# A two-layer attention trunk: compression with both halves stationary, rotary columns once, and weight halves made by GpSimd

## The chip, the core and the metric

One core of a Trainium2 chip runs the whole program. Its engines are TensorE (PE, matrix products; PEld is its weight load), VectorE (DVE), ScalarE (ACT) and GpSimd (POOL); SyncE (SP) issues nearly all transfers from HBM. Each engine takes its instructions strictly in order and waits at an instruction until the semaphores it needs are set. The metric is the device time of one execution in microseconds (us); lower is better.

## What is computed

Two layers over a residual stream of 256 rows by 1024 columns, all in float32. The part of a layer that the change touches is its first, the token mixing; cross-attention over 256 memory rows and a gated FFN with a short convolution follow.

```
h = x @ w_in[l]
cq, ckv, kr, nq, kc, vc, ks, vs, kw, vw, gl = split(h)
# latent attention: 8 heads of 64 plain + 32 rotary columns
q = (rms_norm(cq, cq_g) @ w_uq).reshape(B, S, 8, 96)
q_rope = apply_rope(q[..., 64:], cos, sin)
# sparse attention: 8 heads in 2 groups; its compressed branch
flat = overlapping blocks of 32 rows (stride 16) of kc or vc, plus a position code
kc_, vc_ = gelu(flat @ w1 + b1) @ w2          # 15 blocks, 2 groups, 64 columns
s = q @ kc_.T * scale - slope * distance;  p_c = masked_softmax(s)
o = g0 * (p_c @ vc_) + g1 * selected_branch + g2 * window_branch
mix = concat(o_mla, o_nsa) @ w_out[l];  x = LN(alpha * x + mix)
```

## The kernel before

A float32 product is made of three fast ones: each operand is split into a rounded part hi and a rest lo, and hi*hi + hi*lo + lo*hi are summed in PSUM. So every weight goes through the same steps (`piece`): a transfer into a raw tile, hi by ScalarE (L130), lo = raw - hi by VectorE (L131), and the matmuls. A piece is up to 128 x 1024; there are 4 raw tiles and 6 of hi and of lo. `wmat` cuts a weight into pieces, `mm_nat` (L169 to L171) and `mm_tr` (L177 to L179) issue the three products.

The program is a list of steps for each layer (`attn` in the table CFG). Layer 0 runs: kc, nq1, nq0, par, k, cmp, v, mem, tab, qk0, cq, qk1, cps, ckv, cmt, fill and so on. The list only sets the order in which the steps are written; a scheduler then puts each engine's instructions in an order of its own, which mixes steps. What matters here:

- kc projects the inputs of the compression and splits them into c2 (hi and lo, tiles of their own). cmp (`compress`) multiplies them by w1: for each of two branches (key, value) and 8 slices three matmuls with 34 stationary columns (32 blocks and 2 of the position code) and 256 moving ones (L516 to L518). The result hs (34 x 512) is copied from PSUM by VectorE (L160; the table's option H is 0), transposed in four pieces (L523), copied to ht, and a gelu by its tanh form follows: u, u2, a tanh on ScalarE (L540). gek and gev (L542, L547) are its results; two products with w2 (L552, L554) make the compressed keys kc and values vct.
- v projects values and gates; cq and ckv are the low-rank query and key inputs of the latent attention.
- mem normalizes the two tiles of 128 memory rows, mb: mean and spread by VectorE (or, for one tile, ScalarE), the power -0.5 on GpSimd (`rsqrt`, L209, tiles mv and ss), then on VectorE (x - mean) * g (L239) and times the power plus b (L240), each in two halves of 512 columns.
- tab loads six tables. GpSimd makes the distance table alibi for 8 heads out of neg (L323), 8 instructions.
- cps makes the probabilities of the compressed branch: 32 products of 32 columns (cmps), steps on VectorE, and on GpSimd a subtraction (L657) and a mask (L659). They are stored 32 wide, of which 16 hold values, the rest is set to zero by GpSimd (L667). cmt transposes them in 4 pieces (L675); in av0 to av3 the products with vct (L690) take 32 rows each.
- mq0 to mq3 (`mla_q`) make the query of two heads each. The 32 rotary columns stand twice in the weight, the second time with halves swapped, so that a head fills 128 columns; one multiplication by the table c_cs (L749) evicts both heads, and the score product adds the two rotary parts. That is 18 matmuls of 256 columns for each of four steps.
- fill is work for the next stage (keys and values of the cross-attention, out of the normalized memory), put in where TensorE might wait. pt and pT are transposed attention probabilities, qk the scores.

Of the kernel before, what the change touches and what calls it, by code (L numbers as in the profile page):

```python
# [53 lines left out]
def consts():  # L54
# [1007 lines left out]
```

## Time and profile before

| | us |
|---|---|
| median of 3 runs | 880.95 |
| lowest, highest | 879.26, 881.2 |
| the profiled execution, its own time | 879.98 |
| its span, first to last instruction | 877.9 |
| TensorE busy, share of the span | 860.3, 98% |
| VectorE, ScalarE, GpSimd busy | 665.2, 532.5, 132.4 |
| mean granted TensorE clock, of full speed | 0.993 |

The profile is of one execution; it begins at its first instruction, and 2.1 us of the time lie outside the span. Matmuls are pipelined: the duration of one record (280 ns for 256 columns) is longer than the distance to the next, and only the distance adds to the time. "L" and a number is a line of the kernel. A time in square brackets is how long an engine idled ahead of the row, with what ended the wait. A step on PSUM or SBUF that reads what another engine wrote waits for that engine's semaphore, and all that stands behind it in its queue waits with it.

### The profile page before, as it was taken

Reading aid. Unit: us, or ns where it says so; the run is one execution under the profiler, and the core shown is the slowest. Engines: PE = TensorE matmul, PEld = TensorE weight load, DVE = VectorE, ACT = ScalarE, POOL = GpSimd, SP = SyncE. Lnnn points to the kernel's source line nnn. Section 1 sums busy time; section 2 is a strip of 40 time slices with the busy share of each in tenths; the row PEclk is TensorE's granted clock in tenths of the full one; section 3 lists DMA queues with packets and bytes.
Section 4 is the critical chain, followed back from the end, with each engine's and each line's share of the span. In section 5 each row is a group of like instructions: output and inputs, shape, how many; then the busy total and the mean of one; then the engine's idle time right before and its main releaser. Section 6 shows DMA issues by size and latency. Waiting matters only on the chain.

```text
span 877.9 us, 14948 instructions
## 1 busy us (share of the span) xinstructions
PE 860.3 (98%) x5502; PEld 766.7 (87%) x5502; DVE 665.2 (76%) x1290; ACT 532.5 (61%) x1014; POOL 132.4 (15%) x140
## 2 busy tenths in 40 slices
PE   8989999999999999999999999999999999999996
PEld 5989798899989888888989998879998888888895
DVE  7789887766578877677688788968566877777777
ACT  5658764555546676666555678636573567667661
POOL 1052000000000332222300020000000033223220
PEclk9989999999999999999999999999999999999998
DMA  7944463476347756656538634446633655665641
GB/s 229 284 145 124 132 173 113 140 251 190 96 123 237 217 158 216 190 165 217 183 110 239 190 90 110 144 127 210 194 119 121 218 159 179 212 192 171 215 142 48
DMA packets 128236, 148.66 MB, mean 169 GB/s; under 512 B 6259, under 2 KB 111009, under 8 KB 128163
## 3 DMA queue, kind: packets, MB, share of 16 engines
q1 hardware_dynamic: 128159, 147.70, 54.5%
q8 instruction: 43, 0.70, 0.3%
q14 instruction: 30, 0.25, 0.1%
q10 hardware_dynamic: 4, 0.01, 0.0%
HBM read 146.64 MB, written 1.05 MB: 168 GB/s over the span
## 4 chain that ended last, share of the span: by engine, by line
PE 91%; DVE 4%; ACT 2%; DMA 2%; issue 1%; POOL 0%; SPq 0%; DVEq 0%; ACTq 0%; POOLq 0%
PE up L259 16%; PE up L261 8%; PE acc L996 5%; PE acc L997 5%; PE acc L998 5%; PE acc L170 3%; PE acc L171 3%; PE acc L169 3%; PE fill L178 2%; PE fill L179 2%; PE xq L179 2%; PE xq L178 2%; PE xq L177 2%; PE fill L171 2%; PE fill L169 2%; PE fill L170 2%
## 5 line engine op out<-in xcount | busy, mean ns | idle before, releaser
L131 DVE TENSOR_TENSOR lo<-raw,hi 128x1024 fp32r<-128x1024 f32 (+5 forms) x296 | 322.8, 1108 | 96.2 <-ACT hi L130 94.0
L130 ACT ACTIVATE hi<-raw 128x1024 fp32r<-128x1024 f32 (+5 forms) x296 | 275.8, 951 | 108.9 <-PE acc L171 34.4
L259 PE MATMUL up<-xT,hi 128*128 128x512 f32 x608 | 152.1, 392 | 0.0
L259 PEld LDWEIGHTS up<-xT,hi 128*128 128x128 f32 x608 | 110.3, 189 | 20.3
L261 PEld LDWEIGHTS up<-xT,lo 128*128 128x128 f32 x608 | 82.9, 190 | 5.9
L984 POOL TENSOR_TENSOR cv<-cv 128x256 f32<-128x256 f32 x40 | 54.2, 1356 | 218.7 <-ACT cv L982 170.0
L261 PE MATMUL up<-xT,lo 128*128 128x256 f32 x608 | 84.8, 282 | 0.0
L978 ACT ACTIVATE cv<-u,par 128x256 f32<-128x256 f32 x76 | 45.4, 598 | 49.6 <-DVE u L971 49.6
L996 PE MATMUL acc<-hi,frh 128*128 128x512 f32 x176 | 68.9, 392 | 0.0
L997 PE MATMUL acc<-lo,frh 128*128 128x512 f32 x176 | 68.8, 391 | 0.0
L998 PE MATMUL acc<-hi,frl 128*128 128x512 f32 x176 | 68.2, 389 | 0.0
L209 POOL TENSOR_TENSOR mv<-mv,mhalf 128x1 f32<-128x1 f32 x16 | 14.3, 897 | 309.0 <-DVE mv L233 158.5
L979 DVE SCALAR_TENSOR_TENSOR cv<-u,par,cv 128x255 f32<-128x255 f32 x76 | 37.6, 495 | 26.4 <-ACT cv L978 26.4
L584 ACT ACTIVATE p<-p,nm 128x128 f32<-128x128 f32 x96 | 42.6, 447 | 9.7 <-DVE nm L581 9.4
L986 ACT ACTIVATE frh<-cv 128x256 fp32r<-128x256 f32 x44 | 18.4, 418 | 37.8 <-POOL cv L984 35.4
L987 POOL TENSOR_TENSOR frl<-cv,frh 128x256 fp32r<-128x256 f32 x40 | 38.0, 952 | 20.3 <-ACT frh L986 20.3
L980 DVE SCALAR_TENSOR_TENSOR cv<-u,par,cv 128x254 f32<-128x254 f32 x76 | 37.9, 498 | 2.5
L998 PEld LDWEIGHTS acc<-hi,frl 128*128 128x128 f32 x176 | 33.0, 188 | 7.5 <-DVE frl L987 0.7
L996 PEld LDWEIGHTS acc<-hi,frh 128*128 128x128 f32 x176 | 33.1, 188 | 7.0 <-ACT frh L986 0.9
L997 PEld LDWEIGHTS acc<-lo,frh 128*128 128x128 f32 x176 | 33.1, 188 | 6.0
L177 PE MATMUL fill<-mTh,hi 128*128 128x256 f32 x128 | 37.2, 291 | 0.0
L179 PE MATMUL fill<-mTh,lo 128*128 128x256 f32 x128 | 36.6, 286 | 0.0
(279 smaller groups left out, 2151.7 us busy)
## 6 DMA issues: line engine op xcount, KB each, us to landing
raw<-in_ffn_w_up SPq DMA_DIRECT2D x88, 512.0 KB, 4.4
raw<-in_ffn_w_down SPq DMA_DIRECT2D x44, 512.0 KB, 4.3
raw<-in_xa_wkv SPq DMA_DIRECT2D x32, 512.0 KB, 3.8
raw<-in_xa_wq SPq DMA_DIRECT2D x16, 512.0 KB, 5.4
raw<-in_xa_wo SPq DMA_DIRECT2D x16, 512.0 KB, 4.2
raw<-in_w_in SPq DMA_DIRECT2D x24, 256.0 KB, 3.4
raw<-in_w_out SPq DMA_DIRECT2D x16, 256.0 KB, 4.6
raw<-in_w_out SPq DMA_DIRECT2D x8, 512.0 KB
```

Source lines behind the costliest of these rows:

```text
L130: A.activation(h_, x_, AF.Copy)
L131: V.tensor_tensor(l_, x_, h_.bitcast(F32), op=ALU.subtract)
L169: T.matmul(o, xh_[:, t, k], h, start=k == 0, stop=False)
L177: T.matmul(o, h[:, ms], xh_[:, :, k], start=k == 0, stop=False)
L179: T.matmul(o, lo[:, ms], xh_[:, :, k], start=False, stop=k == len(ws) - 1)
L259: T.matmul(o, h[:, ms], x2[:, k], start=k == 0, stop=False)
L261: T.matmul(o[:, 0:S], lo[:, ms], x2[:, k, 0], start=False, stop=k == len(ws) - 1)
L978: A.activation(c, u, AF.Identity, bias=pcol("cb", l, ft), scale=w_[2])
L984: E.tensor_tensor(conv[0], conv[0], conv[1], op=ALU.mult)
L996: T.matmul(o, fh[:, ts_], h[:, cs_], start=f == 0, stop=False)
L997: T.matmul(o, fh[:, ts_], lo[:, cs_], start=False, stop=False)
L998: T.matmul(o, fl[:, ts_], h[:, cs_], start=False, stop=f == NF - 1)
```

## The change

Four things change in the token mixing of both layers; nothing else does.

1. **Compression.** hi and lo of the inputs lie side by side in one tile, and both are stationary at once, 68 columns in place of 34. Two matmuls for each slice do what three did, 64 in place of 96 in all. (The product lo*lo comes along.) hs has 68 rows, is copied by ScalarE (option H is 1), and its transposes have 68 columns each; ht takes ScalarE's copy of the lo part and an addition on VectorE.
2. **Compressed branch.** Keys and probabilities are 16 wide, all heads of both groups in one set of 128 rows: one value product in place of two (a layer), vct spread over heads by a multiplication with a new table c_half, two transposes in place of four, and no zeroing of the probabilities. The products with vct have 128 rows in place of 32.
3. **Query.** The rotary columns stand once. Each step makes 9 matmuls for the plain columns of two heads; every second step makes 9 more for the rotary columns of four. The eviction is by ScalarE copies for the plain part; for the rotary part by a shuffle, three VectorE steps on 128 x 256 and four copies. c_cs has twice the size. GpSimd clears 32 rows of each query tile.
4. **GpSimd makes lo halves.** In cq, ckv, mkv and fill every second piece's lo is GpSimd's, in mq0 to mq3 every one (L135 and L760 of the new file).

The order of the last steps of the lists becomes mq0 mq1 ... mq2 mq3 in both layers.

```diff
+        share["n"] += share["on"]
+        E = G if share["on"] and share["n"] % 2 else V
...
-            V.tensor_tensor(l_, x_, h_.bitcast(F32), op=ALU.subtract)
+            E.tensor_tensor(l_, x_, h_.bitcast(F32), op=ALU.subtract)
...
+            call = big.tile([P, 2, 2, 272], F32R, name="c2", tag="oTh")
             for j, nm in ((0, "pek"), (1, "pev")):
-                ch, cl = [tmp.tile([P, 272], F32R, name="c2" + s_, tag="pp", bufs=PP) for s_ in "hl"]
+                c = call[:, j]
+                ch, cl = c[:, 0], c[:, 1]
...
-                        o = hid[0:34, j * 256:(j + 1) * 256]
-                        c_h, c_l = ch[:, i:i + 265:8], cl[:, i:i + 265:8]
-                        T.matmul(o, c_h, h[:, i - i0], start=i == 0, stop=False)
-                        T.matmul(o, c_h, lo[:, i - i0], start=False, stop=False)
-                        T.matmul(o, c_l, h[:, i - i0], start=False, stop=i == 7)
+                        o = hid[0:68, j * 256:(j + 1) * 256]
+                        c_hl = c2[j][:, :, i:i + 265:8]
+                        T.matmul(o, c_hl, h[:, i - i0], start=i == 0, stop=False)
+                        T.matmul(o, c_hl, lo[:, i - i0], start=False, stop=i == 7)
...
-            A.activation(ht.rearrange("p a b c -> p (a b c)"), pt[:, 0:136], AF.Copy)
+            A.activation(htf, hp[:, :, 1], AF.Copy)
+            V.tensor_tensor(htf, hp[:, :, 0], htf, op=ALU.add)
...
-            for g in range(2):
-                T.matmul(pc[:, 128 + g * 64:192 + g * 64], gv[:, g].rearrange("p i b -> p (i b)"), w2[:, 2, :],
-                         start=True, stop=True)
+            T.matmul(pc[:, 128:192], gv.rearrange("p j g b -> p (j g b)"), w2[:, 2, :], start=True, stop=True)
...
+            V.tensor_tensor(vct, pc[:, None, 128:192].to_broadcast([P, HN, 64]),
+                            half[:, :, None].to_broadcast([P, HN, 64]), op=ALU.mult)
...
-            pc = st.tile([P, NT, HN, 32], F32, name="pc", tag="pc", bufs=1)
-            G.memset(pc, 0.0)
-            V.tensor_tensor(pc.rearrange("p t h b -> p (t h) b")[:, :, 0:16], f, bc(mx), op=ALU.mult)
+            V.tensor_tensor(f, f, bc(mx), op=ALU.mult)
...
-            for g in range(2):
-                for t in range(NT):
-                    T.transpose(pt[:, g * S + t * P:g * S + (t + 1) * P],
-                                pc[:, t, 4 * g:4 * g + 4, :].rearrange("p h b -> p (h b)"), ident)
+            for t in range(NT):
+                T.transpose(pt[:, t * P:(t + 1) * P], pc[:, t * P:(t + 1) * P], ident)
...
-                T.matmul(po[64 * g:64 * g + 64, 0:S], vct[js, g, :], pct[js, g, :], start=False, stop=True)
+                T.matmul(po[64 * g:64 * g + 64, 0:S], vct[:, 2 * j + g, :], pct, start=False, stop=True)
...
-            for i in range(2):
-                mm_tr(pb[:, i * S:(i + 1) * S], ch[0], ch[1], ws, i * P)
-            j = 2 * (hp % 2)
-            V.tensor_tensor(qT[hp // 2][:, j:j + 2, :], pb.rearrange("p (i n) -> p i n", i=2),
-                            cs[:, None, :].to_broadcast([P, 2, S]), op=ALU.mult)
+            for cut, dh, dl in ((slice(0, 64), h, lo), (slice(64, 96), rh[:, :, ms], rl[:, :, ms])):
+                src, dh, dl = heads(rv)[:, :, :, cut], heads(dh), heads(dl)
+                A.activation(dh, src, AF.Copy)
+                G.tensor_tensor(dl, src, dh.bitcast(F32), op=ALU.subtract)
+            mm_tr(pb[:, 0:S], ch[0], ch[1], [(h[:, k], lo[:, k]) for k in range(3)], 0)
+            if last:
+                mm_tr(pb[:, S:2 * S], ch[0], ch[1], [(rh[:, k], rl[:, k]) for k in range(3)], 0)
+            for j in range(2):
+                A.activation(qT[g][0:64, 2 * i + j, :], pb[64 * j:64 * j + 64, 0:S], AF.Copy)
+            if last:
+                V.stream_shuffle(rs, pb[:, S:2 * S], [(c + 16) % 32 for c in range(32)])
+                V.tensor_tensor(rc, pb[:, S:2 * S], cs[:, 0], op=ALU.mult)
+                V.tensor_tensor(rs, rs, cs[:, 1], op=ALU.mult)
+                V.tensor_tensor(rc, rc, rs, op=ALU.add)
+                for j in range(4):
+                    copy_(qT[g][64:96, j, :], rc[32 * j:32 * j + 32], j % 2)
...
+                for g in range(2):
+                    G.memset(qT[g][96:128], 0.0)
+            share["on"] = name in ("cq", "ckv", "mkv", "fill") or name[:2] == "mq"
```

The scheduler's order shifts with it. The places that matter, in layer 0; numbers behind a name tell tiles of one kind apart. TensorE, from the end of the v projection (proj, 280 columns) to the start of cq (384 columns), before:

```order
L170 MATMUL proj_655<-lo_624,xT_103 128x280
L171 MATMUL proj_655<-hi_623,xT_103 128x280
L169 MATMUL proj_829<-hi_807,xT_103 128x384
L170 MATMUL proj_829<-lo_808,xT_103 128x384
L552 MATMUL cmp_597<-gek_587,w2_593 128x30
L554 MATMUL cmp_597<-w2_593,gev_589 128x64 x2
L171 MATMUL proj_829<-hi_807,xT_103 128x384
```

and now:

```order
L174 MATMUL proj_638<-lo_607,xT_103 128x280
L561 MATMUL cmp_581<-gek_571,w2_577 128x30
L175 MATMUL proj_638<-hi_606,xT_103 128x280
L562 MATMUL cmp_581<-w2_577,gev_573 128x64
L251 MATMUL lnt_685<-c_ident_80,mb_668 128x128 x4
L173 MATMUL proj_812<-hi_790,xT_103 128x384
```

The product with gek has moved up by three matmuls, ahead of the last of the v projection. VectorE, the steps that lead to gek, before (mb is the memory, mv its norms, u2 the gelu's argument):

```order
L239 SCALAR_TENSOR_TENSOR mb_685<-mb_685,mv_716,mg_686 128x512
L538 TENSOR_SCALAR u2_582<-u2_582 128x60
L239 SCALAR_TENSOR_TENSOR mb_685<-mb_685,mv_716,mg_686 128x512
L539 TENSOR_TENSOR u2_582<-u2_582,u_575 128x60
L229 TENSOR_SCALAR mv_691<-mv_691 128x1
L239 SCALAR_TENSOR_TENSOR mb_685<-mb_685,mv_691,mg_686 128x512 x2
L542 SCALAR_TENSOR_TENSOR gek_587<-u2_582,u_575 128x30
```

and now:

```order
L244 SCALAR_TENSOR_TENSOR mb_668<-mb_668,mv_699,mg_669 128x512
L546 TENSOR_TENSOR u2_566<-u_559 128x60
L243 SCALAR_TENSOR_TENSOR mb_668<-mb_668,mv_699,mg_669 128x512
L547 TENSOR_SCALAR u2_566<-u2_566 128x60
L233 TENSOR_SCALAR mv_674<-mv_674 128x1
L243 SCALAR_TENSOR_TENSOR mb_668<-mb_668,mv_674,mg_669 128x512
L548 TENSOR_TENSOR u2_566<-u2_566,u_559 128x60
L244 SCALAR_TENSOR_TENSOR mb_668<-mb_668,mv_674,mg_669 128x512
L551 SCALAR_TENSOR_TENSOR gek_571<-u2_566,u_559 128x30
```

Two steps L244 (L240 before), which multiply by the power, now stand ahead of gek; before, all of that kind stood behind it. GpSimd, from the alibi steps to the compressed probabilities sc, before:

```order
L323 TENSOR_SCALAR alibi_179<-neg_744 128x256 x8
L209 TENSOR_TENSOR mv_716<-mv_716,mhalf_84 128x1
L209 TENSOR_TENSOR mv_691<-mv_691,mhalf_84 128x1
L544 MEMSET gev_5641 128x256
L209 TENSOR_TENSOR ss_855<-ss_855,mhalf_84 128x1
L209 TENSOR_TENSOR ss_886<-ss_886,mhalf_84 128x1
L657 TENSOR_TENSOR sc_954<-sc_954,cmx_957 128x256
L209 TENSOR_TENSOR ss_1013<-ss_1013,mhalf_84 128x1
L659 TENSOR_TENSOR sc_954<-sc_954,c_cok_178 128x256
```

and now:

```order
L328 TENSOR_SCALAR alibi_180<-neg_727 128x256 x8
L213 TENSOR_TENSOR mv_699<-mv_699,mhalf_84 128x1
L135 TENSOR_TENSOR lo_791<-raw_788,hi_790 128x768
L213 TENSOR_TENSOR mv_674<-mv_674,mhalf_84 128x1
L553 MEMSET gev_5606 128x128
L135 TENSOR_TENSOR lo_803<-raw_800,hi_802 128x768
L135 TENSOR_TENSOR lo_953<-raw_950,hi_952 128x864
L135 TENSOR_TENSOR lo_965<-raw_962,hi_964 128x576
L213 TENSOR_TENSOR ss_838<-ss_838,mhalf_84 128x1
L213 TENSOR_TENSOR ss_869<-ss_869,mhalf_84 128x1
L665 TENSOR_TENSOR sc_937<-sc_937,cmx_940 128x256
L135 TENSOR_TENSOR lo_1058<-raw_1055,hi_1057 128x1024
```

Halves of weights stand between the two powers of the memory, and one of 1024 columns between the two steps of the probabilities. On SyncE's queue, the fifth piece of w_in, 512 KB, was issued ahead of the layer's parameters and now is issued behind them; neg follows later in the same queue in both.

## Rows read from the trace of the kernel before

**Rows 1.** page, 1: engine, busy us (share), instructions; 4: the chain's shares

```profile
PE 860.3 (98%) x5502; PEld 766.7 (87%) x5502; DVE 665.2 (76%) x1290; ACT 532.5 (61%) x1014; POOL 132.4 (15%) x140
...
PE 91%; DVE 4%; ACT 2%; DMA 2%; issue 1%; POOL 0%; SPq 0%; DVEq 0%; ACTq 0%; POOLq 0%
```

**Rows 2.** TensorE's waits: engine line <- what ended it: us, times, longest

```profile
PE cmp L523 <- DVE hs L160: 4.0, 2, 3.2
...
PE pt L597 <- ACT pT L600: 1.4, 3, 0.6
```

**Rows 3.** stretches: us, busy us of PE, PEld, DVE, ACT, POOL, clock, DMA share, GB/s

```profile
20.00:30.00 10.00, 10.00 (x86) 10.00 (x85) 7.98 (x15) 5.94 (x12) 0.00 (x0) 1.00 0.97 262
...
46.30:50.70 4.40, 1.28 (x11) 1.05 (x8) 4.28 (x8) 3.06 (x5) 4.40 (x5) 0.88 0.88 271
...
52.00:54.00 2.00, 2.00 (x10) 2.00 (x10) 2.00 (x10) 1.50 (x3) 1.94 (x2) 0.50 0.84 245
54.00:56.50 2.50, 2.50 (x13) 2.50 (x12) 2.50 (x7) 1.04 (x5) 2.27 (x4) 0.51 0.68 227
...
500.00:502.00 2.00, 1.23 (x11) 1.17 (x11) 1.79 (x6) 0.29 (x1) 0.00 (x0) 1.00 0.92 243
```

**Rows 4.** timeline of TensorE, layer 0: start, us, engine, line, op, out<-in

```profile
50.77 0.64 PE L523 MATMUL cmp<-c_ident,hs 34*128 34x34 f32 x4 [3.18 <-DVE hs L160]
...
59.24 0.30 PE L552 MATMUL cmp<-gek,w 128*128 128x30 f32 x2
...
84.50 0.60 PE L675 MATMUL cmpt<-c_ident,pc 128*128 128x128 f32 x4
84.85 0.36 PE L177 MATMUL fill<-mTh,hi 128*128 128x256 f32 x1
```

**Rows 5.** stretch of the compression's matmuls alone: us, busy (x), clock, DMA, GB/s

```profile
40.70:46.30 5.60, 5.60 (x48) 1.00 0.96 308
```

**Rows 6.** timelines of SyncE's queue and of GpSimd, layer 0

```profile
38.76 0.51 SPq L321 DMA_DIRECT2D neg<-in_c_neg  x1
...
45.03 10.03 POOL L323 TENSOR_SCALAR alibi<-neg 128x256 bf16<-128x256 f32 x8 [32.32 <-DMA neg<-in_c_neg]
55.14 1.28 POOL L209 TENSOR_TENSOR mv<-mv,mhalf 128x1 f32<-128x1 f32 x2
...
77.49 0.63 POOL L657 TENSOR_TENSOR sc<-sc,cmx 128x256 f32<-128x256 f32 x1 [3.42 <-DVE cmx L655]
...
79.98 0.73 POOL L659 TENSOR_TENSOR sc<-sc,c_cok 128x256 f32<-128x256 f32 x1
```

**Rows 7.** timeline of VectorE, layer 0

```profile
50.03 0.68 DVE L160 COPY hs<-cmp 34x512 f32<-34x512 f32 x1
...
58.17 0.19 DVE L542 SCALAR_TENSOR_TENSOR gek<-u,u 128x30 f32<-128x30 f32 x1 [1.50 <-ACT u L540]
58.27 0.34 DVE L547 SCALAR_TENSOR_TENSOR gev<-u,u 128x60 f32<-128x60 f32 x2
58.54 0.75 DVE L240 SCALAR_TENSOR_TENSOR mb<-mb,mv,mg 128x512 f32<-128x512 f32 x1
```

**Rows 8.** groups by form: line, engine, op, tiles, x; busy us, mean ns

```profile
L984 POOL TENSOR_TENSOR cv<-cv 128x256 f32<-128x256 f32 x40 | 54.2, 1356 | 218.7 <-ACT cv L982 170.0 <-PE up L259 48.7
L987 POOL TENSOR_TENSOR frl<-cv,frh 128x256 fp32r<-128x256 f32 x40 | 38.0, 952 | 20.3 <-ACT frh L986 20.3
...
L435 POOL TENSOR_TENSOR kr<-m 128x32 f32<-128x32 f32 x4 | 1.6, 404 | 6.1 <-DVE m L433 6.1
L657 POOL TENSOR_TENSOR sc<-sc,cmx 128x256 f32<-128x256 f32 x2 | 1.3, 626 | 51.2 <-DVE sm L588 47.8 <-DVE cmx L655 3.4
...
L131 DVE TENSOR_TENSOR lo<-raw,hi 128x1024 fp32r<-128x1024 f32 x228 | 280.5, 1240 | 93.5 <-ACT hi L130 91.4 <-PE up L963 0.7
```

More of the change, by code (lines that the diff above doesn't have):

```diff
@@ L73, in consts @@
     ok = np.broadcast_to(ok, (P, NT, HN, 16))
-    ctab = np.where(ok, -(slopes * 8.0)[None, None, :, None] * (t - cend), -BIG).astype(f)
+    order = np.arange(HN).reshape(2, 4).T.reshape(-1)
+    ctab = np.where(ok, -(slopes[order] * 8.0)[None, None, :, None] * (t - cend), -BIG).astype(f)
+    half = np.repeat(0.5 * np.eye(HN, dtype=f), 16, 0)
     return {
-        "c_ident": ident, "c_neg": neg, "c_tri": tri, "c_cs": cs, "c_kcs": np.ascontiguousarray(kcs),
+        "c_ident": ident, "c_neg": neg, "c_tri": tri, "c_cs": np.ascontiguousarray(cs), "c_kcs": np.ascontiguousarray(kcs),
@@ L115, in trunk @@
     RAW, HL, PP = SIZES
+    share = {"on": False, "n": 0}
     def piece(nk, n, segs, wn=None, cols=None):
@@ L316, in trunk @@
     cok = const.tile([P, NT, HN, 16], F32, name="c_cok", tag="c_cok")
+    half = const.tile([P, HN], F32, name="c_half", tag="c_half")
     alibi = const.tile([P, HN, S], BF16, name="alibi", tag="alibi")
@@ L745, in mla_q @@
-            pb = bank("mla")
-            for i in range(2):
-                mm_tr(pb[:, i * S:(i + 1) * S], ch[0], ch[1], ws, i * P)
-            j = 2 * (hp % 2)
-            V.tensor_tensor(qT[hp // 2][:, j:j + 2, :], pb.rearrange("p (i n) -> p i n", i=2),
-                            cs[:, None, :].to_broadcast([P, 2, S]), op=ALU.mult)
+            g, i = divmod(hp, 2)
+            last = g in rw
+            if not last:
+                rw[g] = [wp.tile([P, 3, P], F32R, name="r" + s, tag=s, bufs=HL) for s in ("hi", "lo")]
@@ new lines, in mla_q @@
+            rh, rl = rw[g]
+            r = wp.tile([P, 1024], F32, name="raw", tag="raw", bufs=RAW)
+            rv = r[:, :576].rearrange("p (k n) -> p k n", k=3)
+            nc.sync.dma_start(rv, a["mla_w_uq"][l][:, hp * 192:(hp + 1) * 192].rearrange("(k p) n -> p k n", p=P))
+            h, lo = [wp.tile([P, 3, P], F32R, name=s, tag=s, bufs=HL) for s in ("hi", "lo")]
+            heads = lambda v: v.rearrange("p k (h c) -> p k h c", h=2)
+            ms = slice(64 * i, 64 * i + 64)
+            for cut, dh, dl in ((slice(0, 64), h, lo), (slice(64, 96), rh[:, :, ms], rl[:, :, ms])):
+                src, dh, dl = heads(rv)[:, :, :, cut], heads(dh), heads(dl)
+                A.activation(dh, src, AF.Copy)
+                G.tensor_tensor(dl, src, dh.bitcast(F32), op=ALU.subtract)
@@ L794, in trunk @@
             "ckv": in_ckv,
-            "par": lambda: load_params((0,)),
+            "par": lambda: (load_params((0,)), nc.sync.dma_start(half, a["c_half"])),
             "par2": lambda: load_params((1, 2, 3)),
```

54 lines of the change are left out of this document (26 added, 28 removed).

## The prediction

> **What bounds the kernel now.** First the busy table and the chain of work that ended last [rows 1]: TensorE is busy for 860.3 of 877.9 us and carries 91% of the chain; GpSimd is busy for 15% and carries none of it. So a matmul that goes is worth its spacing wherever TensorE's queue is full, and nothing where the next instruction waits for another engine. Next, TensorE's list of waits [rows 2]: the largest by far is the four transposes of the compression's hidden layer, which wait for hs, 4.0 us in two places, 3.2 of it in layer 0. The windows round that place [rows 3] show a second price: the granted clock is 1.00 in 20 to 30 us, 0.88 while TensorE idles, and 0.50 from 52 to 54, that is 1.2 in place of 2.4 GHz, after the engine had stood; layer 1's shorter wait at 500 leaves 1.00. Last, the timelines of TensorE, GpSimd and VectorE from 45 to 60 us [rows 4, 6, 7], since that is where the change puts new instructions into queues that are served in order.
>
> **Direct savings on TensorE.** Compression: 48 matmuls of 256 columns fill 5.60 us of a layer [rows 5], 0.117 us each; 16 of 48 go, 1.9 us in each layer. The query: 72 become 54 a layer, and I take the same size of matmul at the same spacing: 18 x 0.117 = 2.1 us a layer. The transposes of the compressed probabilities: four stand from 84.50 to 84.85 [rows 4], 0.09 us each, two go, 0.2. The value product behind gek loses two of four matmuls, shorter still; at the same price 0.2. The eight products with 128 rows in place of 32 keep their number and their columns. Sum 4.4 us a layer, 8.8 in all, 1.0% of the time. Now what lies behind each.
>
> **Layer 0, to the start of cq.** Before, hs is copied by VectorE at 50.03 [rows 7], behind pieces of weights, and its transposes start at 50.77 after 3.18 us of idling [rows 4]. ScalarE now copies it, behind the key evictions only, so up to 3.2 us of idling, up to 2.8 us of slow clock (some 5.7 us at half rate, from 50.8 to 56.5 [rows 3, 4]), the 1.9 of the compression and about 0.5 at the start (the first piece's lo no longer stands ahead of x) become free: TensorE would reach the end of the v projection near 50.5 in place of 58.9. But the product with gek stands ahead of the last v matmul, in TensorE's order. gek is now behind five steps that normalize the memory, on VectorE; two of these (L244) wait for GpSimd's powers, and those stand behind eight alibi steps. Before, gek came ahead of all steps that need a power, at 58.17, and VectorE took the first of them at 58.54 [rows 7].
> By rows, with the table neg landing as before: alibi 45.03 to 55.06 [rows 6]; the first power 0.64 (1.28 for two), to 55.8; on VectorE then three mb steps of 0.75 and four small ones that follow each other at 0.1 as gek and gev do (58.17, 58.27) [rows 7], to 58.5; GpSimd meanwhile a lo half of 768 columns and the second power. That half has no row on GpSimd. The nearest: a plain two-operand step of 128x32 takes 404 ns and one of 128x256 with an fp32r result 952 [rows 8]; that is 2.45 ns a column and 326 ns fixed, 2.2 us for 768. So power two ends near 58.7, mb takes 0.75, gek 0.19, and TensorE goes on near 59.8. The equal point before is L552's start at 59.24 [rows 4] less two cq matmuls of 384 columns ahead of it (1.5 x 0.117 each): 58.9. So 0.9 late. Besides, 512 KB of w_in that were issued ahead of the parameters are now issued behind them, and neg's issue at 38.76 [rows 6] is behind that: at 262 GB/s [rows 3] 2.0 us if no hole in the DMA takes them up, 0 if all; I take 1.0. So +1.9 (bounds 0.3 to 2.9). TensorE has then stood some 9 us, longer than the 3.2 after which the clock was at half; I take the same 2.8 us of slow running, now under cq (bounds 0 and 2.8). Layer 0 stands at **+4.7** where cq is under way, and the compression's gain, the wait's and the start's are in it already.
>
> **Layer 0, the rest.** The value product gives 0.2 and the query 2.1 back; the compressed probabilities lose 0.2 of transposes. Their chain has a new link: GpSimd's subtraction (77.49) and its mask (79.98) [rows 6] now have a whole lo half of 1024 between them, 2.45 x 1024 + 326 ns = 2.8 us. Before, a power stood there, and TensorE idled 1.4 us in all for pT [rows 2], some of it at this place. The transposes now stand ahead of 48 fill matmuls that could have covered for them. I take +1.2 (bounds -1 and +3). VectorE loses the lo halves (a 1024 one takes 1240 ns there [rows 8]), and so some of its lateness; the bound of -1 is for that. The query's lo halves of 384 and 192 columns (1.3 and 0.8 us), the shuffle and the rotary steps run while TensorE has other heads' work queued: nothing. Layer 0: 4.7 - 2.5 + 1.2 = **+3.4**.
>
> **Layer 1.** No alibi and no memory norm stand in the way here. The 4.4 are saved; hs stands behind ScalarE's two key copies, I take 0.5 more wait than the 0.8 of before (4.0 less 3.2 [rows 2]), since TensorE arrives 1.9 earlier at a copy that starts little earlier (bounds -0.8 and +1.4), and 0.5 for two powers of the query's norm behind lo halves (bounds 0 and 1.5). Layer 1: **-3.4**. Cross-attention and FFN keep their instructions and their order.
>
> **Sum:** +3.4 - 3.4 = 0.0. The profiled execution took 879.98 (span 877.9 and 2.1 outside), 1.0 under the median of 880.95. I put the time at **879.9**, against either not to be told from no change: 0.2%, about what a measurement of this kernel can tell, is 1.8 us.
>
> **Where the skill speaks against it.** The row: a lo half of 1024 columns takes VectorE 1240 ns, and GpSimd by my line 2.8 us, 2.3 times that. The Trainium skill, GPSIMD Engine Reference, "Elementwise — side-by-side cycle accounting", gives a ratio of 1.96 for a two-operand step and keeps to VectorE for elementwise work; by it, as an estimate, the 1024 half takes 2.4 and the 768 one 1.9 us, and the sum would be 0.7 lower.
>
> **Rivals.**
> *A, as worked out*, 879.9 (877.5 to 882): chance 0.40, of which 0.07 under the same-band, 0.27 in it, 0.06 over.
> *B, layer 0 keeps part of its gain*: neg lands as early as before (-1.0) or the clock does not fall after this stand (-2.8): both give 876.1. For it: holes in the DMA before 18 us, and that the sum of my bounds there is one-sided. Against it: the 0.50 of rows 3 came after a shorter stand. Chance 0.25.
> *C, gek is not late at all*: alibi steps take the 626 ns of GpSimd's quick row instead of 1245 (10.03 for eight [rows 6]), 5.0 us less, so that TensorE stands about 4 us, or the order lets it pass. -5.0, with -2.8 and the probabilities' +1.2 gone, gives 871. The eight alibi steps are unchanged, which speaks against it. Chance 0.07.
> *D, slower: GpSimd's halves are slow beside VectorE.* The same 128x256 step has a row of 626 ns, between two softmax steps, and one of 1356 in the FFN, where VectorE runs throughout [rows 8]; at the second rate 768 columns take 4.1 and 1024 take 5.4. Then power two is 1.9 later, the mask 2.6 later, and in layer 1 two halves of 512 ahead of a power cost 2.2 more, of which about 1.5 shows: +6.0, 885.9. It decides from where the 1024 half takes over 3.5 us: (768 + 1024 + 1024) x 0.7 ns = 2.0 us, which is 0.2%. The Trainium skill, GPSIMD Engine Reference, "Specifications", has GpSimd share its SBUF interfaces with VectorE and contend with its two-operand steps; the two rows agree with that. For it: VectorE is busy for 76% and mainly with two-operand steps. Against it: the 952 of the FFN's frl step, in the same company. Chance 0.28, of which 0.02 stays within 0.2%.
>
> **Numbers.** Faster by over 0.2%: 0.07 + 0.25 + 0.07 = 0.39. Within: 0.27 + 0.02 = 0.29. Slower: 0.06 + 0.26 = 0.32. The likeliest case's own range is 877.5 to 882; the range 872 to 887 takes in B and most of D, and leaves out C and D's far end.
>
> **What would show it.** In the changed profile, TensorE's list of waits has the product with gek (now L561) as its longest entry, some 7 to 10 us, put down to VectorE, and hs no longer leads. The window behind it shows 0.50. GpSimd's first lo half of 768 stands between two powers right behind alibi, at about 2.2 us. The compression's 32 matmuls a layer stand at 0.117. From the end of layer 0's attention on, everything is some 3 us later than before, and from the end of layer 1's attention on about equal. It is wrong if no wait for gek shows (then C), if the granted clock stays at 1.00 behind it (B), or if lo rows on GpSimd have means of 3.5 us and more for 1024 columns (D).

## The result, and the profile after

The changed kernel takes 887.59 us (median of 885.52 to 887.87), the kernel before beside it 880.11 (878.17 to 881.2): a ratio of 1.0082, 95% interval 1.0057 to 1.0108. It is slower by some 7 us, and the forecast of 879.9 and its range (872 to 887) are both missed. The profiled execution is the quickest of its four: it took 885.52, with a span of 883.7, so the traces have 5.8 us of the loss to explain. Of all executions below one, of all_but_share_in_layer_1, is slow (2939.95 us) and is left out of that run's median.

The busy table, as in [rows 1]:

```profile
PE 851.4 (96%) x5426; PEld 758.6 (86%) x5426; DVE 660.0 (75%) x1272; ACT 539.7 (61%) x1032; POOL 171.1 (19%) x172
```

TensorE is busy for 8.9 us less, close to the 8.8 that the sum of direct savings gave. But its idle time has grown from 17.6 us (877.9 less 860.3) to 32.3. TensorE's waits (us in total, times, longest), against [rows 2]:

```profile
PE pv L614 <- ACT pT L608: 7.1, 5, 2.2
PE cmp L561 <- DVE gek L551: 6.5, 2, 6.2
PE cmpt L680 <- POOL kr L440: 3.7, 1, 3.7
```

Of the 4.0 us for hs 0.4 is left, in layer 1; three waits of 17 us in all have come. Windows of layer 0 (columns as in [rows 3]):

```profile
51.00:57.20 6.20, 0.01 (x1) 0.00 (x0) 4.87 (x10) 1.26 (x3) 3.66 (x4) 0.78 0.24 71
57.20:59.00 1.80, 1.74 (x8) 1.74 (x9) 1.28 (x6) 0.99 (x4) 0.33 (x2) 0.50 0.00 0
59.00:61.00 2.00, 2.00 (x9) 1.90 (x8) 2.00 (x4) 1.41 (x2) 2.00 (x1) 0.50 0.22 49
85.00:87.00 2.00, 2.00 (x11) 2.00 (x12) 1.98 (x1) 0.00 (x0) 2.00 (x2) 0.54 0.77 268
87.00:89.00 2.00, 2.00 (x12) 2.00 (x12) 0.35 (x3) 0.75 (x2) 0.96 (x4) 0.61 0.65 215
```

Behind the 6.2 us stand, and again behind the 3.7 us stand at 81 to 85, the granted clock is at its lower level, 1.2 GHz, for some 4 us each. The second spell is new: (1 - 0.54) x 2 + (1 - 0.61) x 2 = 1.7 us of work lost.

Where the time went is best read from the starts of the same matmuls in TensorE's timelines (us from the span's start; norm_behind_cq, all_but_share_in_layer_1 and "both", which is norm_behind_cq_and_dve_evictions, are experiments, below):

| first matmul of | before | after | norm_behind_cq | both | all_but_share_in_layer_1 |
|---|---|---|---|---|---|
| layer 0, cps (cmps) | 72.63 | 73.08 | 78.08 | 75.39 | 72.95 |
| layer 0, kr or query (mla) | 105.02 | 112.41 | 107.94 | 106.75 | 105.33 |
| layer 0, w_out (acc) | 144.63 | 149.46 | 144.97 | 143.78 | 144.93 |
| layer 0, turn for the norm behind it (lnt) | 170.11 | 175.55 | 171.06 | 169.87 | 170.45 |
| layer 1, kc (projt) | 469.57 | 475.05 | 470.57 | 469.34 | 469.94 |
| layer 1, compress (cmp) | 492.61 | 498.09 | 493.61 | 492.38 | 492.98 |
| layer 1, v (proj) | 498.29 | 502.28 | 497.80 | 496.57 | 497.17 |
| layer 1, mla | 543.71 | 547.93 | 543.46 | 542.24 | 542.22 |
| layer 1, acc | 567.63 | 574.23 | 569.71 | 566.73 | 566.70 |
| layer 1, lnt | 597.59 | 603.18 | 598.71 | 594.58 | 594.55 |

A row compares like with like only where the same work stands ahead of it. In norm_behind_cq and in both, 31 matmuls of ckv have moved ahead of cps, in the changed kernel 2; so their cps row tells nothing of the norm, and the rows from mla on do.

To cps in layer 0 the change costs 0.45 us; from there to mla 6.9 more; from mla to acc it wins 2.6; the last stretch of the mixing takes 0.6 more. Layer 0 is 5.4 late at its lnt and stays so through cross-attention and FFN. Layer 1, from kc to lnt, takes 128.13 in place of 128.02: its saving is lost inside the layer.

### The profile page after: what moved, and what is told of

It reads as the page before. It is cut to its first block, busy times and chain, and to the rows that moved or that the text cites. A ratio compares the mean times of both kernels' runs of the same rounds, so it can differ in the third digit from the quotient of the medians.

```text
span 883.7 us, 14843 instructions
## 1 busy us (share of the span) xinstructions
PE 851.4 (96%) x5426; PEld 758.6 (86%) x5426; DVE 660.0 (75%) x1272; ACT 539.7 (61%) x1032; POOL 171.1 (19%) x172
## 4 chain that ended last, share of the span: by engine, by line
PE 86%; DVE 4%; ACT 3%; POOL 2%; DMA 2%; issue 2%; SPq 0%; DVEq 0%; ACTq 0%; POOLq 0%
PE up L263 16%; PE up L265 8%; PE acc L1025 4%; PE acc L1027 4%; PE acc L1026 4%; PE acc L174 3%; PE acc L173 3%; PE acc L175 3%; PE fill L182 2%; PE fill L181 2%; PE fill L183 2%; PE fill L173 2%; PE fill L175 2%; PE xq L181 2%; PE xq L183 2%; PE xq L182 2%
## 5 line engine op out<-in xcount | busy, mean ns | idle before, releaser
L135 DVE TENSOR_TENSOR lo<-raw,hi 128x1024 fp32r<-128x1024 f32 (+3 forms) x258 | 304.7, 1193 | 95.4 <-ACT hi L134 93.5
L134 ACT ACTIVATE hi<-raw 128x1024 fp32r<-128x1024 f32 (+4 forms) x272 | 267.7, 998 | 110.0 <-PE acc L175 35.2
L592 ACT ACTIVATE p<-p,nm 128x128 f32<-128x128 f32 (+1 forms) x96 | 42.5, 446 | 5.5 <-DVE nm L589 5.1
L135 POOL TENSOR_TENSOR lo<-raw,hi 128x768 fp32r<-128x768 f32 (+4 forms) x14 | 27.2, 1948 | 57.6 <-ACT hi L134 57.3
```

Of the source, the lines that this page charges most:

```text
L135: E.tensor_tensor(l_, x_, h_.bitcast(F32), op=ALU.subtract)
```

## The experiments

The theory at first (O): each part saves on TensorE what it should, and new positions in the in-order queues cost more. Rivals: GpSimd's halves hold up the others (G, rival D in a wider form), or a part does not save at all.

**One part alone, in the kernel before.** Each takes the hunks of one part out of the change:

```
only_compress: two matmuls per slice, hs by ScalarE
+ T.matmul(o, c_hl, h[:, i - i0], ...); T.matmul(o, c_hl, lo[:, i - i0], ...)
+ copy_(hs, hid[0:68, :], cfg['opt']['H'])      # H = 1
only_branch: one 128-row compressed branch
+ T.matmul(pc[:, 128:192], gv..., w2[:, 2, :], ...)
only_query: query without duplicated columns, its list of steps
+ A.activation(qT[g][0:64, 2 * i + j, :], pb[64 * j:64 * j + 64, 0:S], AF.Copy)
only_share: halves of some weights on GpSimd
+ E = G if share["on"] and share["n"] % 2 else V
```

> The kernel before with the first part alone (hi and lo stationary at once, hs copied by ScalarE). Both theories: the wait for hs goes, the matmuls of the compression save 3 us in all (they stand 0.131 us apart in the changed kernel, not 0.117, so 64 x 0.131 in place of 96 x 0.117 = 2.8). gek stands behind two steps that need a power here too, so the wait for gek takes its place in layer 0. Theory O (each part is harmless, the loss comes from the order that they make together): 874 to 878. Theory G (GpSimd's lo halves make the loss): the same, 874 to 878, since none are here.

Measured 882.47, ratio 1.0016 (1.0002 to 1.0030): over the range of both theories by 4 us. The wait for hs has not gone (2.7 us in layer 0), the one for gek is 0.4, and scores, turns and pv wait for pT, for VectorE and for pT (1.7, 1.4 and 1.3 us).

> The kernel before with the second part alone (one compressed branch of 128 rows). Saves 4 transposes and 2 value products, 0.8 us; gek and the transposes keep their place behind other matmuls. Theories O and G: 878.5 to 880.5.

Measured 879.36, 0.9987 (0.9973 to 1.0000), as both theories had it.

> The kernel before with the third part alone (rotary columns once; lo halves of the query's weights on GpSimd, ScalarE evicts the plain parts). Saves 36 matmuls, 4.3 us. Theory O: ScalarE's evictions of the query delay pT at the end of layer 1 by themselves, some 3.5 us back: 878 to 880. Theory G: the small lo halves on GpSimd are late and TensorE waits for them: 880 to 884, with a wait of mla for GpSimd in the list. If neither: 875 to 877.

Measured 882.7, 1.0027 (1.0009 to 1.0046). The time is in G's range, but G's sign is missing: no wait of TensorE is put down to GpSimd. In layer 1 pv waits 3.6 us for pT, as O had it.

> The kernel before with the fourth part alone (every second lo half of cq, ckv, mkv, fill and all of mq on GpSimd). No matmul goes. Theory G: at least half of the loss is here, 883 to 889, with the probabilities' transposes waiting for a chain through GpSimd. Theory O: 879 to 883.

Measured 896.47, 1.0172 (1.0145 to 1.0198): far over both ranges. TensorE waits longest for gek (4.8 us) and at the probabilities' transposes (2.8 and 1.9).

No part alone gains more than 0.13%, and the four do not add up: 0.16 - 0.13 + 0.27 + 1.72 = 2.0% against the 0.82 of all together. By the starts of matmuls, at layer 0's lnt the four stand at +3.2, +1.3, +1.4 and +9.1 us; layer 1 (before 128.02) takes 126.05, 126.87, 129.29 and 132.92. So compression and branch do save 2.0 and 1.2 in layer 1, and every part costs in layer 0.

**All parts but one.** The lines of the part are those of before. (The query's own halves, L760, are part of the query and stay on GpSimd.)

```
all_but_share
- E.tensor_tensor(l_, x_, h_.bitcast(F32), op=ALU.subtract)
+ V.tensor_tensor(l_, x_, h_.bitcast(F32), op=ALU.subtract)
all_but_query: mla_q and the table c_cs of before
```

> The changed kernel with every lo half of cq, ckv, mkv and fill back on VectorE (the query's stay on GpSimd). Theory G (GpSimd's halves make the loss in the combination too): 878 to 882. Theory S (the parts' times add up as measured alone, +1.4, -0.7 and +2.4 us): 883. Theory O (the order does it: the probabilities' transposes stand ahead of all transposes of pT, whoever makes the lo halves): 886 to 889, with a wait of the transposes of 3 us and more in layer 0.

Measured 885.9, 1.0063 (1.0039 to 1.0086): just under O's range, over those of G and S; within the uncertainty, the change without shared halves loses as much as with them. Its waits (columns as above), with 1.9 us at the transposes where O had 3 and more:

```profile
PE pv L611 <- ACT pT L605: 5.9, 4, 2.2
PE cmp L558 <- DVE gek L548: 5.1, 1, 5.1
PE cmpt L677 <- DVE sc L671: 1.9, 1, 1.9
```

The same three waits stand there with no half of cq or fill on GpSimd. So these halves, the 15 us of only_share notwithstanding, are not what makes the loss of the whole. (They do lengthen the wait for gek, 6.2 us with them; how is told below.)

> The changed kernel with the query as before (duplicated rotary columns, one VectorE multiplication to evict). Theory Q (at the end of the attention ScalarE's evictions of the query delay pT, 3.7 us in layer 1 and 1.0 in layer 0, and eat the 4.2 saved): both go, 887 to 888, with no wait of pv for pT over 1.3 us in layer 1. If the query gains in this combination: 890 and more. If it costs more than that: 885 and less.

Measured 887.43, 1.0072 (1.0049 to 1.0094), as theory Q had it. In layer 1 pv waits only 0.21 us for pT, so those waits come with the query. In this company, though, TensorE waits 3.4 us for one of GpSimd's halves (L137, layer 0), as in no other run.

**The probabilities' turn behind the fill, and the query evicted by VectorE.** Each is the changed kernel with one edit:

```
cmt_behind_fill
- cps ckv cmt fill av0
+ cps ckv fill cmt av0
query_evicted_by_dve
- A.activation(qT[g][0:64, 2 * i + j, :], pb[64 * j:64 * j + 64, 0:S], AF.Copy)
+ V.tensor_copy(qT[g][0:64, 2 * i + j, :], pb[64 * j:64 * j + 64, 0:S])
```

> The changed kernel with the probabilities' transposes of layer 0 written behind the fill step, so that TensorE has 48 matmuls ahead of them. Theory W (the wait of 3.7 us and the slow clock behind it, 4 us at about half rate, are a loss of their own): 5.4 us less, 881.5 to 883.5. Theory M (the wait only moves, to the next product that needs the transposed probabilities): 886.5 to 889.

Measured 886.85, 1.0071 (1.0052 to 1.0091). The wait at L680 is gone, and one for pT of 3.1 us stands at the next turn: it only moved, as theory M had it.

> The changed kernel with the plain query columns copied by VectorE in place of ScalarE. Theory Q: pT is no longer behind these copies in ScalarE's queue, the waits of pv for pT in layer 1 (2.2 and 1.5 us) and at 133 us in layer 0 (1.0) go: 882.5 to 884.5. If VectorE, which has four lo halves of 1024 there, is late instead: 886 to 889, with waits for VectorE.

Measured 887.83, 1.0083 (1.0065 to 1.0102). Layer 1 takes 125.19 in place of 128.13, so ScalarE's evictions did cost it 2.9; but layer 0 lost 5 us in the same run, and the total hides both. Of these 5, 1.9 stand at cps (the wait for gek is 7.6 in place of 6.2) and 3.1 between mla and w_out, where TensorE waits 1.0 for a transfer of parameters and a spell of half clock takes 1.7. That the edit makes these is not shown.

**The memory's norm at another place in layer 0's list**, in the changed kernel (first two) and in the kernel before:

```
norm_behind_tables
- par k cmp v mem tab qk0 cq qk1
+ par k cmp v tab mem qk0 cq qk1
norm_behind_cq, before_norm_behind_cq
- par k cmp v mem tab qk0 cq qk1
+ par k cmp v tab qk0 cq mem qk1
```

> The changed kernel with one step moved in layer 0's list: the memory's norm (mem) stands behind the tables (tab). In the build the two products with the compressed key (L551, L556) then stand ahead of the norm's last multiplications (L244) on VectorE, while the turn of the probabilities (L680) is still behind one of the twelve pt turns only. Theory that the in-order queues' order makes the loss: the 6.2 us wait of TensorE for gek falls to under 3.5 us, the waits at the probabilities (3.7 us, then about 3.6 us for pT) stay, and the time is 882 to 885. Rival, that GpSimd's and ScalarE's shared work sets the start of layer 0 and not the order: gek stays 5 us or more late, or what is gained is waited for at the next step, 885 to 888.

Measured 885.49, 1.0057 (1.0038 to 1.0075), with the executions spread from 881.16 to 886.3; the profile shows the quickest. In it the wait for gek is 2.7 and the others stand as the theory had them:

```profile
PE pv L614 <- ACT pT L608: 7.0, 5, 2.2
PE cmpt L680 <- POOL kr L440: 3.6, 1, 3.6
PE cmp L561 <- DVE gek L551: 3.0, 2, 2.7
PE lnt L251 <- DVE mb L244: 2.1, 1, 2.1
```

But the last row is new: 2.1 of the 3.5 won at gek is waited for at the norm, as the rival had it, and the median is 0.5 above the theory's range. gek's place alone is not the cure. (The profiled execution is the one whose clock did not fall; the last section has it.)

> The changed kernel with the memory's norm placed behind the projection cq in layer 0's list. In the build gek then follows its own chain on VectorE with no L244 ahead of it, and all twelve pt turns and three of the score matmul groups stand ahead of the probabilities' turn (L680), as in the kernel before. Theory of the queues' order: both waits go, gek under 3.5 us and L680 under 1 us, with no pT wait over 1 us in the 20 us behind; layer 0 is at its end 3 to 6 us earlier than in the changed kernel, 880 to 883. Layer 1 keeps its 3.7 us of pT waits. Rival of the late probabilities as such (their chain on VectorE, GpSimd and ScalarE ends late wherever they stand): a wait of 2 us or more remains at L680 or at what reads its result, 884 to 887.

Measured 881.55, 1.0027 (1.0015 to 1.0038): 0.55% of the 0.82 come back, 4.8 us. Its waits:

```profile
PE cmp L561 <- DVE gek L551: 3.6, 2, 3.3
PE pv L614 <- ACT pT L608: 3.2, 2, 2.2
...
PE lnt L251 <- DVE mb L244: 2.0, 2, 1.2
```

None is left at L680. Turns and scores ahead of it wait 1.3 and 1.1 us for pT where none over 1 was expected, and of layer 1's pT waits only the 2.2 is left, not 3.7; layer 1 takes 128.14 all the same, with a spell of half clock in it. The move mends gek's place and the turns' at once. Against norm_behind_tables, which mends gek's alone, the turns' place is worth 1.0057 less 1.0027, 0.3% or some 2.6 us; the two intervals meet at 1.0038, and how much of it is the clock's fall no run separates.

> The kernel before with the memory's norm behind cq in layer 0's list. Theory that the place repairs what the change broke, and that the kernel before had nothing to repair (no wait for gek, 0.3 us or less at the probabilities): no gain, 879.5 to 883, with new waits for the norm (mb) of some 2 us as in the changed kernel. Rival, that the place is better for any kernel: 873 to 877, and then the change as such still costs what it did.

Measured 882.0, 1.0039 (1.0025 to 1.0053): in the kernel before the same move costs 0.4%. The place is not better as such; it repairs what the change broke.

**Layer 1 alone changed**, layer 0 as before. A layer picks its functions:

```
+ fns = dict(in_kc=in_kc_n if l else in_kc, compress=compress_n if l else compress, ...)
all_but_share_in_layer_1, besides: branch and query of the change if l,
+ V.tensor_copy(qT[g][0:64, 2 * i + j, :], pb[64 * j:64 * j + 64, 0:S])
```

> The kernel before, with the [hi|lo] stationary of the compression in layer 1 alone; layer 0 is as before. Theory that the direct saving is real and only layer 0's order eats it: layer 1 is 1.5 to 2 us shorter, the time is 878.0 to 879.0 beside a kernel before of 880 to 880.5. Rival, that the part saves nothing wherever it stands (the clock falls for the shorter stretch, the next chain is late): 879.8 to 881.

Measured 878.23, 0.9983 (0.9973 to 0.9993), and layer 1 takes 126.08, 1.9 less than before: as the theory had it.

> The kernel before, with compression, compressed branch and query changed in layer 1 alone, the query's evictions (L766) on VectorE in place of ScalarE, no halves shared; layer 0 is as before but for two table loads on SP behind its parameters. Theory that the direct savings are real and add up where no queue's order turns against them: layer 1 is 2.5 to 4.5 us shorter from the projection of the key to ln1, the time 876 to 878. Rival, that in layer 1 the query's saving is lost to pT whoever evicts, and the rest to the lower clock behind short waits: 878.5 to 881.

Measured 875.64, 0.9955 (0.9940 to 0.9971): faster than both kernels. (Its query's halves are on GpSimd; no weight of `piece` is.) Layer 1 takes 124.61 from kc to lnt, 3.4 less than before: the savings are there and add up where no queue turns against them.

**Both cures together**, in both layers of the changed kernel: the norm behind cq, and VectorE's evictions in layer 1 only; then without shared halves:

```
+ if l: V.tensor_copy(qT[g][0:64, 2 * i + j, :], pb[64 * j:64 * j + 64, 0:S])
+ else: A.activation(qT[g][0:64, 2 * i + j, :], pb[64 * j:64 * j + 64, 0:S], AF.Copy)
```

> The changed kernel with the memory's norm behind cq in layer 0 and the query's evictions (L766) on VectorE in layer 1 alone. If the two causes are separate and add up: 3 us less than with the norm's place alone (881.6), so 878 to 879.5, layer 1's pT waits of 2.2 and 1.4 us under 0.5 each. If layer 1's waits only change their place: 880.5 to 882.

Measured 878.35, 0.9987 (0.9970 to 1.0004).

> The same without the halves on GpSimd (all on VectorE). If these halves cost or gain little in company, as the change without them (885.9 beside 887.6) says: within 1.5 us of the run with them, 877 to 880. If they make the rest of layer 0's loss: 875 to 877. If they are what keeps VectorE free there: 880 to 884.

Measured 879.27, 1.0000 (0.9986 to 1.0013). The two cures are separate and add up, from 1.0082 over 1.0027 to 0.9987, and the shared halves again make no difference in time that the intervals tell. With both cures the change is level with the kernel before; layer 0 still does not gain (169.87 at lnt against 170.11), and TensorE still waits in it for gek, mb and pT (2.9, 0.8 and 1.3 at the longest). Without the shared halves the waits stand elsewhere: 0.7 for gek, but 2.5 at the probabilities' transposes, with 15 turns ahead of them. So turns ahead do not always cover that wait.

## Why the prediction was wrong, step by step

**The direct savings: nearly right, the equality in part by luck.** 8.8 forecast, 8.9 less busy. The busy time after holds 3.6 us of slow running, by the windows above, where before it held the 2.8 of the prediction, and one term was too large. The compression's 32 matmuls, row of the changed kernel as [rows 5] of before:

```profile
40.07:44.25 4.18, 4.18 (x32) 4.18 (x32) 0.00 (x0) 0.00 (x0) 1.00 0.99 348
```

4.18 / 32 = 0.131 us, not 0.117, so a layer saves 5.68 - 4.19 = 1.5 (layer 1) and not 1.9. Loading 68 stationary columns takes 220 ns where 34 took 143; that this is why the matmuls stand further apart is not shown.

**Layer 0's start: right place, size 4 us too high.** The wait for gek is there, 6.2 us (7 to 10 were told), with gek right behind L244 and that behind GpSimd's second power; it was priced at +4.7 by the time cq runs, and cps stands at +0.45. GpSimd and VectorE (start, duration, idle ahead):

```profile
44.04 7.16 POOL L328 TENSOR_SCALAR alibi<-neg 128x256 bf16<-128x256 f32 x8 [31.92 <-DMA neg<-in_c_neg]
51.28 0.56 POOL L213 TENSOR_TENSOR mv<-mv,mhalf 128x1 f32<-128x1 f32 x1
51.81 1.80 POOL L135 TENSOR_TENSOR lo<-raw,hi 128x768 fp32r<-128x768 f32 x1
55.20 1.13 POOL L213 TENSOR_TENSOR mv<-mv,mhalf 128x1 f32<-128x1 f32 x1 [1.58 <-DVE mv L233]
```

```profile
56.36 0.75 DVE L244 SCALAR_TENSOR_TENSOR mb<-mb,mv,mg 128x512 f32<-128x512 f32 x1 [0.45 <-POOL mv L213]
57.03 0.18 DVE L551 SCALAR_TENSOR_TENSOR gek<-u,u 128x30 f32<-128x30 f32 x1
```

neg landed 1.0 earlier than before [rows 6], not 1.0 later, and alibi took 7.16 in place of 10.03: rivals B and C each came in part. TensorE went on at 57.26, not at 60.8. The slow clock did come, as expected. The prediction had GpSimd's half hold up the second power. It did not: it ended at 53.61, and the power then idled 1.58 for VectorE. But VectorE was slow beside it. The first L244, here and (second row, L241) in all_but_share, which has no half there:

```profile
51.88 2.28 DVE L244 SCALAR_TENSOR_TENSOR mb<-mb,mv,mg 128x512 f32<-128x512 f32 x1 [4.05 <-POOL mv L213]
```

```profile
52.66 0.75 DVE L241 SCALAR_TENSOR_TENSOR mb<-mb,mv,mg 128x512 f32<-128x512 f32 x1 [4.05 <-POOL mv L210]
```

2.28 against 0.75: 1.5 us on the way to gek that the prediction did not have, though its time for the half was near (1.80, 2.2 told).

**The rest of layer 0: the step that failed.** It gave +1.2 for the probabilities, with -1 to +3 as bounds; from cps to mla the change costs 6.9. The start's error, the other way, hid 4 us of this. TensorE's timeline there:

```profile
80.98 0.27 PE L605 MATMUL pt<-c_ident,p 128*128 128x128 f32 x1
84.97 0.49 PE L680 MATMUL cmpt<-c_ident,sc 128*128 128x128 f32 x2 [3.73 <-POOL kr L440]
85.14 0.55 PE L181 MATMUL fill<-mTh,hi 128*128 128x256 f32 x1
...
92.49 0.71 PE L605 MATMUL pt<-c_ident,p 128*128 128x128 f32 x5
93.82 0.89 PE L605 MATMUL pt<-c_ident,p 128*128 128x128 f32 x6 [0.62 <-DVE nm L589]
95.91 0.81 PE L614 MATMUL pv<-pT,vsl 128*64 128x256 f32 x3 [1.19 <-ACT pT L608]
...
100.81 0.88 PE L605 MATMUL pt<-c_ident,p 128*128 128x128 f32 x6 [0.64 <-ACT pT L608]
...
104.30 0.43 PE L614 MATMUL pv<-pT,vsl 128*64 128x256 f32 x1 [1.20 <-ACT pT L608]
```

The profile names kr on GpSimd as the releaser, but the step that L680 reads, the last multiplication of sc on VectorE, ends at 84.83:

```profile
84.07 0.76 DVE L674 TENSOR_TENSOR sc<-sc,cmx 128x256 f32<-128x256 f32 x1
```

The matmul is 0.5 later than before (L675 at 84.50 [rows 4]); the half of 1024 columns on GpSimd is in that chain, and all_but_share, without it, still waits 1.9. What changed most is TensorE's order. Before, between ckv and L675:

```profile
80.79 0.82 PE L597 MATMUL pt<-c_ident,p 128*128 128x128 f32 x6
82.23 0.93 PE L597 MATMUL pt<-c_ident,p 128*128 128x128 f32 x6 [0.62 <-ACT pT L600]
83.45 0.74 PE L616 MATMUL qk<-kk,qs 128*128 128x256 f32 x4 [0.30 <-DVE nm L581]
84.03 0.63 PE L635 MATMUL qk<-kk,qs 128*128 128x512 f32 x2
```

Twelve turns pt and six score matmuls stood ahead of L675 and filled the time; now one turn does, the other eleven and the scores stand behind 48 fill matmuls, and their copies pT come late for pv. That is 3.7 of wait, 3.65 of smaller ones behind it and 1.7 of slow clock, less 1.2 us of waits that the kernel before has in the same stretch and 0.2 for the turns saved: 7.65, of which 6.9 shows. The prediction named the fill as cover that now stands behind, but the fill stood behind L675 before, too (84.85 [rows 4]); what had moved were the turns and scores, and it asked only how late the chain would be and not what TensorE would still have ahead of it. It had no slow clock at this place either. norm_behind_cq puts the turns back ahead of L680, and layer 0 is 4.5 us earlier, with gek's wait mended in the same move; cmt_behind_fill shows that moving the transposes alone moves the wait.

**The query's work at "nothing": wrong.** The prediction put its halves, shuffle and rotary steps at nothing and did not name ScalarE's plain evictions at all. These cost layer 1 2.9 us, nearly the 2.1 + 1.5 that it saves. ScalarE and TensorE there:

```profile
559.74 0.76 ACT L766 ACTIVATE qT<-mla 64x256 f32<-64x256 f32 x2
560.52 2.01 ACT L134 ACTIVATE hi<-raw 128x1024 fp32r<-128x1024 f32 x2
562.55 0.77 ACT L766 ACTIVATE qT<-mla 64x256 f32<-64x256 f32 x2
563.35 0.87 ACT L608 ACTIVATE pT<-pt 128x384 f32<-128x384 f32 x2
566.28 1.06 ACT L134 ACTIVATE hi<-raw 128x1024 fp32r<-128x1024 f32 x1 [2.07 <-DMA raw<-in_w_out]
567.37 0.84 ACT L162 ACTIVATE qT<-rc 32x256 f32<-32x256 f32 x2
568.23 0.87 ACT L608 ACTIVATE pT<-pt 128x384 f32<-128x384 f32 x2
```

```profile
563.89 0.81 PE L614 MATMUL pv<-pT,vsl 128*64 128x256 f32 x3 [2.18 <-ACT pT L608]
...
568.77 0.81 PE L614 MATMUL pv<-pT,vwn 128*64 128x256 f32 x3 [1.48 <-ACT pT L608]
```

ScalarE works without a gap from 559.74 to 564.22: four evictions take 1.5 us, two halves of pieces 2.0, and pT, whose turns TensorE ran from 560.24 on, stands behind them all. The second pT stands behind a piece of w_out, for whose transfer ScalarE idles 2.07 us, and behind copies of the rotary part. The prediction said what TensorE had queued meanwhile, but not what stood behind the new evictions on ScalarE. That they are the cause is shown by query_evicted_by_dve: with that one edit layer 1 takes 125.19 in place of 128.13, and the pT waits of 2.2 and 1.5 are gone. So layer 1 came to +0.1 and not to -3.4. With the evictions on VectorE and no shared halves it comes to -3.4.

**Rival D gave nearly the time (885.9), but not by its mechanism.** It needed a 1024 half of over 3.5 us. What came is the reverse, a VectorE step slow beside GpSimd's half, 1.5 us of it ahead of gek. Groups of the changed kernel (busy us, mean ns):

```profile
L135 POOL TENSOR_TENSOR lo<-raw,hi 128x768 fp32r<-128x768 f32 x4 | 7.8, 1956 | 3.3 <-ACT hi L134 3.3
L135 POOL TENSOR_TENSOR lo<-raw,hi 128x1024 fp32r<-128x1024 f32 x3 | 7.2, 2395 | 7.4 <-ACT hi L134 7.4
```

2395 and 1956 ns, under the 2.8 and 2.2 us of the line through two far rows. The Trainium skill's ratio of 1.96 (GPSIMD Engine Reference, "Elementwise — side-by-side cycle accounting") had given 2.4 and 1.9 as an estimate: the trace agrees with the page.

**The sum.** Forecast +4.7, -1.3, -3.4; measured +0.45, +5.0, +0.1 at the same places, and 0.25 in the stages behind the mixing: 5.8, the difference of the spans. (The medians differ by 7.5; the rest lies between executions, and no trace shows where.) So everything is 5.4 later from the end of layer 0's mixing, where 3 was told, and 5.6 from that of layer 1's, where about 0 was. The range failed because the bound of +3 took the probabilities' lateness for the whole price of their place.

What stays open: why only_share alone loses 15 us, how much of layer 0's loss is the clock's fall and not the waits, and why layer 0 does not gain even with both cures. The last would need an order written for the new durations.

## What to carry to other kernels

When a change shortens work on the bounding engine ahead of an in-order wait, the saving is paid back at the wait unless what it waits for moves too: list what each engine has ahead of and behind every such instruction, before and after, and price the work that lost its place as cover. An eviction given to another engine is not free because that engine is idle on average; it is priced by what stands behind it there. And try a change in the stage where it has room: nearly the same edits gain 0.45% in layer 1 alone, while the whole change loses 5.4 us in layer 0.

## What the runs showed of the hardware

**GpSimd's steps go by VectorE's company.** The eight alibi steps, the same in all kernels, over their own stretch, in the kernel before, in the changed one and in only_compress (columns as in [rows 3]):

```profile
45.03:55.06 10.03, 6.85 (x41) 6.55 (x40) 9.90 (x21) 6.06 (x10) 9.84 (x8) 0.73 0.85 254
```

```profile
44.04:51.20 7.16, 6.97 (x55) 6.60 (x54) 3.69 (x12) 5.13 (x11) 6.97 (x8) 1.00 0.74 260
```

```profile
44.30:52.51 8.21, 5.55 (x35) 5.33 (x35) 7.11 (x17) 5.97 (x13) 8.02 (x8) 0.82 0.78 244
```

VectorE busy for 99%, 52% and 87% of the stretch goes with means of 1245, 887 and 1018 ns. Not every step is longer: the medians are 1000, 848 and 910 ns, and the longest one took 2482, before. The prediction held them fixed, as "unchanged". The Trainium skill, GPSIMD Engine Reference, "Specifications", says that GpSimd's interfaces to SBUF are shared with VectorE; these rows agree. It goes the other way, too: VectorE's step L244 that began at 51.88, 0.07 after a half on GpSimd, took 2.28 us and ended at 54.16, 0.55 after that half. In only_share the same step (L243 there) began at 62.65 beside a half of 864 columns, took 1.86 and ended 0.54 after it. In all_but_share, with no half beside it, it took 0.75.

**The clock's fall is not the same in each execution.** In the profiled execution of norm_behind_tables the clock stays at 1.00 behind a 3.6 us wait at L680 (columns as above):

```profile
82.00:84.00 2.00, 1.72 (x15) 1.75 (x16) 1.90 (x3) 0.27 (x1) 2.00 (x3) 1.00 0.82 195
84.00:86.00 2.00, 2.00 (x19) 2.00 (x18) 0.65 (x4) 0.75 (x2) 1.02 (x3) 1.00 0.70 217
```

That execution took 881.16 at a mean clock of 0.998; the five others of the same program took 883.23 to 886.3 at 0.992 to 0.994. So one program can take some 4 us more or less, and a single profile of such a kernel may show either. In the profiled execution layer 0 ends at 171.33, only 0.3 behind norm_behind_cq's, with the waits at L680 and pT still there. The other five have no trace: that the clock fell at the same wait in them is likely by their mean clocks, but not shown.
